# Two spreading transfers moved behind weight splits on ScalarE, and row products asked 0.9 sooner, in a hybrid decoder layer

## The chip, the cores and the metric

The kernel runs on 1 core of a Trainium2 chip. The metric is device time of one launch in microseconds (us); lower is better. The kernel before takes 1327.38 us, the median of 3 runs between 1325.91 and 1329.63.

The engines are named as the profile names them: PE is TensorE (matrix products), PEld its weight loads, DVE is VectorE, ACT is ScalarE, POOL is GpSimd, SP is SyncE. An engine name with a q (SPq, ACTq) is that engine's instruction queue where it issues a transfer (DMA). Each engine works through its own instructions in order, and engines wait for one another on semaphores.

## The reference

One decoder layer on 512 tokens of width 1024, in float32: a gated FFN, a mixer (a state-space scan with 16 heads in 4 groups beside differential attention with 8 heads), attention into a fixed memory of 256 rows, and a second gated FFN. Cut to the parts that the change touches:

```python
# differential attention: a learned bias per bucket of relative position, per head
bias = jnp.transpose(rel_bias[rel_bucket(rel)], (2, 0, 1))
logits = jnp.einsum('bqhcd,bkhcd->bhcqk', q_blk, k) * scale
logits = logits + bias[None, :, None]

# scan branch: a group norm over each of the 4 groups of channels
y = y.reshape(bsz, seqlen, SSD_WIDTH) * jax.nn.silu(z)
yg = y.reshape(bsz, seqlen, SSD_GROUPS, SSD_WIDTH // SSD_GROUPS)
yg = yg * lax.rsqrt(jnp.mean(yg * yg, axis=-1, keepdims=True) + EPS)

x = x + 0.5 * swiglu(rms_norm(x, norm_ffn1_w[l]), ffn1_w_in[l], ffn1_w_out[l])   # first FFN
```

## The kernel before

**Products in three passes.** Every large product takes both operands apart into a high and a low part and runs three passes on TensorE (high by high, low by high, high by low). A weight tile of 128x1024 (or 128x512) comes by a transfer from SyncE into one of six `wr` buffers; ScalarE writes the high part `wh` (L155), VectorE the low part `wl` (L156). This pair is called a weight split; three buffers each hold their results. TensorE can use a weight only when its split is done.

**The FFNs** use seven block products in place of eight. Some of them need sums of weight blocks. In the first FFN these sums are made on the way: GpSimd issues a second transfer that adds another block onto a `wr` buffer just loaded (L1290, "accumulating transfer"), or VectorE adds two loaded blocks (L1300, L1341). `out_blocks` (L1243) is the second half of a third of the FFN: seven products named here by their right operands, in the order "11" into `oa`, S1 into `oe`, S2 into `ob`, "12" into `oa`, S3 into `ob`, S4 into `oe`, "22" into `ob`. Each has, for the last third (3 tiles of the hidden width), a first part of 12 matmuls with a 128x1024 weight and a second part of 6 with a 128x512 weight; each part's split is asked for when the part begins. `recent` (L180, L1260) always holds the two instructions of the weight split asked for last.

**The order of the work.** A planner written by hand (`Order`, L57) emits the program. The dense products are one long generator; around them run chains (`spawn`), generators that yield how much later they want to go on. The planner's clock `od.t` advances with the matmuls emitted, by (columns + 8)/2400 us each for the three-pass kind and four times that for a plain float32 product. A chain resumes at the first step of the dense work at which its time has come. The numbers in `W` (L38 to L40) are such yields. SyncE's and GpSimd's instructions keep the order in which they are emitted (L104); the other engines' instructions are put in order by a scheduler that works from its own estimate of times and from data dependences. `tc.issue_after(i)` adds an order edge: what is traced inside it comes behind `i` on `i`'s engine; the kernel's helper `behind(ins)` (L184) does that for a list.

**The position table.** `prepare` (L604) is a chain spawned when the last third's `out_blocks` begins (`beside(2)`, L555). It loads the 32x8 table and a 32x512 one-hot matrix `hot`, and after 9.0 multiplies them on TensorE (`prel`, L614). After 1.5 ScalarE scales the result into `hot` (L619); after 2.0 ScalarE issues two small transfers to a table `rel_d` in device memory (L622, 8 KB each); after 6.0 it calls `expand_bias(S, hd)` for heads 0 and 1. `expand_bias` (L628) issues one transfer from the given queue that spreads a head's row of 640 values over 128 rows of `rel_z` (L629, 320 KB), from which `ask_bias` (L728) later reads a skewed 128x512 tile. The other six heads' spreads go out on SyncE in `queries_keys` (L738).

**The group norm.** `group` (L889) is a chain, one for each of the four groups of scan channels. At its end it sums squares with TensorE (`pn`), takes the root on GpSimd, waits `W["gn"]`, and calls `row_of(rh, 4, G, G, W["gr"])` (L992): VectorE splits the four columns, GpSimd makes two 128x512 diagonal tiles (`ndiag`, L368), the chain yields `W["gr"]`, and TensorE multiplies them by ones (`nrow`, L373, the "row products"). VectorE then scales `y` (L995), which is split for the output projection (`ysh`, `ysl`).

Of the kernel before, what the change touches and what calls it, by code (L numbers as in the profile page):

```python
# [35 lines left out]
LEAD = 4  # L36

W = {"h0": 3.4, "hs": 3.3, "hv": 2.08, "hp": 6.75}  # L38
W |= {"g0": 8.28, "gc": 0.75, "gx": 0.92, "gb": 2.59, "gs": 0.51, "gt": 2.0, "gd": 6.9, "gy": 0.38, "gq": 11.8, "gn": 1.5, "gr": 5.3}
W |= {"c0": 4.97, "cs": 3.0, "ct": 4.82}  # L40

SPLIT, AHEAD = 5, 2
# [58 lines left out]
def body(tc, a, dbg=None):  # L101
# [25 lines left out]
    def small(s, n, bufs=None):  # L127
        return tiny.tile([P, n], F32, tag=s, name=nm(s), bufs=bufs)
# [4 lines left out]
    def aux(s, shape=(P, T)):  # L133
        return aux_p.tile(list(shape), F32, tag="aux", name=nm(s))
# [5 lines left out]
    last, start, last_sum, recent, newest, newest_mm = [], [], [], [], [], []  # L140
    V, S, G = nc.vector, nc.scalar, nc.gpsimd
    od = Order()

    def mm(out, w, x, start, stop):
        od.t += (1 if w.dtype == R32 else 4) * (x.free_size() + 8) / 2400
        newest_mm[:] = [nc.tensor.matmul(out, w, x, start=start, stop=stop).ins]  # L146
# [36 lines left out]
    @contextmanager  # L183
    def behind(ins):  # L184
        with ExitStack() as after:
            for i in ins:
                after.enter_context(tc.issue_after(i))
            yield
# [361 lines left out]
    def beside(ti):  # L550
        if ti == 0:
            od.spawn(lambdas())
        elif ti == 1:
            od.spawn(early())
        elif ti == 2:  # L555
            od.spawn(prepare())
            od.spawn(memory_in(hm), 1.0)
# [46 lines left out]
    def prepare():  # L604
        rel_sb = small("rel_sb", 8, bufs=1)[:NUM_BUCKETS]
        nc.sync.dma_start(rel_sb, a["rel_bias"])
        for i in range(2):
            nc.sync.dma_start(hot[i], a["hot"][:, i * H : (i + 1) * H])
        rel_far = small("rel_far", 64, bufs=1)[:8]
        V.memset(rel_far, MASKED)  # L610
        yield 9.0
        prel = aux("prel", (8, T))
        for i in range(2):
            mm(prel[:, i * H : (i + 1) * H], rel_sb, hot[i], True, True)  # L614
        for c in range(T, RW, 64):
            S.dma_start(rel_d[:, c : c + 64], rel_far)
        yield 1.5
        for i in range(2):
            S.activation(hot[i][:8], prel[:, i * H : (i + 1) * H], AF.Copy, scale=-8.0)  # L619
        yield 2.0  # L620
        for i in range(2):
            S.dma_start(rel_d[:, i * H : (i + 1) * H], hot[i][:8])  # L622
        hot.clear()
        yield 6.0
        for hd in range(2):
            expand_bias(S, hd)

    def expand_bias(queue, hd):  # L628
        queue.dma_start(rel_z[hd, :, :RW], rel_d[hd : hd + 1].to_broadcast([P, RW]))  # L629
# [885 lines left out]
```

## Time and profile before

| | |
|---|---|
| median of 3 runs | 1327.38 us (1325.91 to 1329.63) |
| the profiled execution | 1329.7 us, of which the span of instructions is 1327.5 |
| mean granted TensorE clock | 0.991 |
| PE busy | 1298.4 us (98%) |
| DVE / ACT / POOL busy | 987.1 / 708.5 / 123.2 us |
| weight splits, ACT L155 | 329 of 1020 ns |
| weight splits, DVE L156 | 329 of 1174 ns |
| the two spreads from ScalarE, issue to landing | 5.4 us (median) |

In the profile, a row of the timeline or of the chain of waits has start, length, engine, line, operation, output<-inputs, count, and in brackets the idle time before it with what ended it. A row of the waits has the waiting engine, the line, what it waited for, then total, count and longest in us. A row of the stage table has the stretch, its length, then each engine's busy time (with its count), the granted TensorE clock as a share of full speed, the busy share of the 16 DMA engines and GB/s. Buffer numbers are left out of names.

### The profile page before, as it was taken

How to read it: one execution, taken by the hardware profiler on the slowest of the kernel's cores; microseconds unless marked ns; L12 is line 12 of the kernel's file. 1: busy time of each engine (PE TensorE's matmuls, PEld its weight loads, DVE VectorE, ACT ScalarE, POOL GpSimd, SP SyncE). 2: the span in 40 equal slices, each digit the busy share in tenths (PEclk: the TensorE clock that was granted, in tenths of full speed). 3: DMA queues.
4: the chain of work that ended last, by engine and by line, in shares of the span. 5: the costliest groups of instructions: out<-in, count | busy, mean ns of one | idle time of the engine just before them, and what ended most of it. 6: DMA issues, size and time to landing. Idle time of an engine off the chain costs nothing.

```text
span 1327.5 us, 20129 instructions
## 1 busy us (share of the span) xinstructions
PE 1298.4 (98%) x7724; PEld 1129.5 (85%) x7724; DVE 987.1 (74%) x1564; ACT 708.5 (53%) x1192; POOL 123.2 (9%) x143
## 2 busy tenths in 40 slices
PE   9999999998899999999999999999999999999996
PEld 7898998897787778777788877888889999989995
DVE  7988788787786586547867877645678878877886
ACT  6544555465654465336654556434465645555564
POOL 0001000010110011110111121120001000000001
PEclk9999999998899999999999999999999999999999
DMA  7567766885794533763465648775238876666752
GB/s 272 159 175 211 178 170 182 233 229 140 234 317 141 153 71 99 252 185 96 96 164 190 177 116 254 201 191 159 63 113 241 212 229 179 188 197 177 199 192 85
DMA packets 70127, 236.33 MB, mean 178 GB/s; under 512 B 8256, under 2 KB 9760, under 8 KB 69680
## 3 DMA queue, kind: packets, MB, share of 16 engines
q1 hardware_dynamic: 54352, 183.20, 40.8%
q0 software_dynamic: 12880, 44.62, 19.2%
q10 hardware_dynamic: 2800, 7.23, 1.7%
q8 instruction: 60, 0.98, 0.3%
q14 instruction: 35, 0.29, 0.1%
HBM read 232.87 MB, written 50.91 MB: 214 GB/s over the span
## 4 chain that ended last, share of the span: by engine, by line
PE 91%; DVE 3%; DMA 2%; ACT 1%; issue 1%; POOL 0%; ACTq 0%; POOLq 0%; DVEq 0%
PE qb L240 12%; PE pm L146 10%; PE qe L240 8%; PE qa L240 8%; PE pxbc L146 7%; PE ob L1270 6%; PE oe L1270 4%; PE oa L1270 4%; PE pq L146 4%; PE pk L146 3%; PE pcq L146 3%; PE pz L146 3%; PE pv L146 3%; PE pck L146 2%; PE pa L146 2%; DMA wr<-in_f1b 2%
## 5 line engine op out<-in xcount | busy, mean ns | idle before, releaser
L155 ACT ACTIVATE wh<-wr 128x1024 fp32r<-128x1024 f32 (+1 forms) x329 | 334.8, 1020 | 378.7 <-issue 66.5
L156 DVE TENSOR_TENSOR wl<-wr,wh 128x1024 fp32r<-128x1024 f32 (+1 forms) x329 | 385.3, 1174 | 151.9 <-ACT wh L155 149.7
L146 PE MATMUL pxbc<-hnh,wh 128*128 128x512 f32 x128 | 52.2, 408 | 0.0
L146 PE MATMUL pxbc<-hnh,wl 128*128 128x512 f32 x128 | 50.3, 393 | 0.0
L146 PE MATMUL pxbc<-hnl,wh 128*128 128x512 f32 x128 | 50.2, 392 | 0.0
L763 ACT ACTIVATE ec<-ec,mn 128x512 f32<-128x512 f32 (+3 forms) x64 | 35.4, 555 | 24.1 <-DVE mn L762 24.1
L240 PE MATMUL qe<-s31h,wl 128*128 128x256 f32 x152 | 43.1, 283 | 0.0
L240 PE MATMUL qa<-h11h,wh 128*128 128x256 f32 x152 | 43.1, 283 | 0.0
L240 PE MATMUL qb<-s24h,wh 128*128 128x256 f32 x152 | 43.0, 283 | 0.0
L240 PE MATMUL qb<-s24l,wh 128*128 128x256 f32 x152 | 43.0, 283 | 0.0
L240 PE MATMUL qb<-s24h,wl 128*128 128x256 f32 x152 | 43.0, 283 | 0.0
L240 PE MATMUL qa<-hmh,wh 128*128 128x256 f32 x152 | 43.0, 283 | 0.0
L240 PE MATMUL qa<-hml,wh 128*128 128x256 f32 x152 | 43.0, 283 | 0.0
L240 PE MATMUL qa<-hmh,wl 128*128 128x256 f32 x152 | 43.0, 283 | 0.0
L240 PE MATMUL qe<-s24h,wh 128*128 128x256 f32 x152 | 43.0, 283 | 0.0
L240 PE MATMUL qe<-s24l,wh 128*128 128x256 f32 x152 | 43.0, 283 | 0.0
L240 PE MATMUL qe<-s24h,wl 128*128 128x256 f32 x152 | 43.0, 283 | 0.0
L240 PE MATMUL qb<-hmh,wh 128*128 128x256 f32 x152 | 43.0, 283 | 0.0
L240 PE MATMUL qb<-hml,wh 128*128 128x256 f32 x152 | 43.0, 283 | 0.0
L240 PE MATMUL qb<-hmh,wl 128*128 128x256 f32 x152 | 43.0, 283 | 0.0
L240 PE MATMUL qa<-h11h,wl 128*128 128x256 f32 x152 | 43.0, 283 | 0.0
L240 PE MATMUL qa<-h11l,wh 128*128 128x256 f32 x152 | 43.0, 283 | 0.0
(448 smaller groups left out, 4184.3 us busy)
## 6 DMA issues: line engine op xcount, KB each, us to landing
wr<-in_f2q SPq DMA_DIRECT2D x44, 512.0 KB, 4.4
wr<-in_f1q SPq DMA_DIRECT2D x40, 512.0 KB, 4.5
wr<-in_f1b SPq DMA_DIRECT2D x30, 512.0 KB, 4.7
isum<-in_f2q SPq DMA_DIRECT2D x22, 512.0 KB, 5.9
wr<-isum SPq DMA_DIRECT2D x22, 512.0 KB, 4.7
wsum<-in_f2b SPq DMA_DIRECT2D x20, 512.0 KB, 6.1
wr<-wsum SPq DMA_DIRECT2D x20, 512.0 KB, 4.6
wr<-in_f1q POOLq DMA_DIRECT2D x16, 512.0 KB, 7.2
```

Source lines behind the costliest of these rows:

```text
L146: newest_mm[:] = [nc.tensor.matmul(out, w, x, start=start, stop=stop).ins]
L155: S.activation(hi, src, AF.Copy),
L156: V.tensor_tensor(lo, src, hi.bitcast(F32), ALU.subtract),
L240: newest_mm[:] = [nc.tensor.matmul(out, a_[:, wc], b_, start=first and f == 0 and kp == 0 and j == 0, stop=kp == n - 1 and j == 2, skip_gr ...
L763: S.activation(ec[:, :n], ec[:, :n], AF.Exp, bias=mn, scale=-1.0, accum_out=sm[c][:, i : i + 1])
L1270: newest_mm[:] = [nc.tensor.matmul(ps, a_[:, ts], b_[:, ws], start=first and k == 0 and j == 0, stop=k == n - 1 and j == 2, skip_group_che ...
```

## The change

`prepare`'s two calls of `expand_bias` now stand inside `behind(list(recent))`: each transfer is put behind the weight split asked for last at the time when it is emitted (its ScalarE half, since the transfer is issued by ScalarE). After each call the chain yields 4.0, so that the second is emitted at least 4.0 of the planner's time later. And `W["gr"]` falls from 5.3 to 4.4: the row products of the group norm are asked 0.9 of the planner's time sooner.

```diff
-W |= {"g0": 8.28, "gc": 0.75, "gx": 0.92, "gb": 2.59, "gs": 0.51, "gt": 2.0, "gd": 6.9, "gy": 0.38, "gq": 11.8, "gn": 1.5, "gr": 5.3}
+W |= {"g0": 8.28, "gc": 0.75, "gx": 0.92, "gb": 2.59, "gs": 0.51, "gt": 2.0, "gd": 6.9, "gy": 0.38, "gq": 11.8, "gn": 1.5, "gr": 4.4}
...
         hot.clear()
         yield 6.0
         for hd in range(2):
-            expand_bias(S, hd)
+            with behind(list(recent)):
+                expand_bias(S, hd)
+            yield 4.0
```

## Prediction

> **What bounds the kernel now.** I read the busy totals, then the chain that ended last as one line, to learn which engine to watch.
>
> ```profile
> PE 1298.4 (98%) x7724; PEld 1129.5 (85%) x7724; DVE 987.1 (74%) x1564; ACT 708.5 (53%) x1192; POOL 123.2 (9%) x143
> PE 91%; DVE 3%; DMA 2%; ACT 1%; issue 1%; POOL 0%; ACTq 0%; POOLq 0%; DVEq 0%
> ```
>
> TensorE is the bound nearly everywhere; ScalarE has 47% of the span to spare. The change adds and removes no instruction and no byte, so it can pay only where TensorE idles or runs at a lower clock. The waits of TensorE and of SyncE's queue say where (us in total, times, longest):
>
> ```profile
> PE oa L1270 <- ACT wh L155: 4.4, 2, 4.0
> PE pq L146 <- DVE vl L156: 3.1, 1, 3.1
> SPq L1251 <- DMA rel_d<-hot: 17.2, 1, 17.2
> ```
>
> The longest TensorE wait inside the kernel, 4.0 us, is for a weight split in the last output stage of the first FFN, where `prepare` works; the next, 3.1 us, comes right behind a group's row products. Both edits aim at a stall. The stage table shows the first (length, PE busy, PEld, DVE, ACT, POOL, granted clock, DMA share, GB/s):
>
> ```profile
> 320.00:324.19 4.19, 0.17 (x2) 0.01 (x1) 0.76 (x3) 1.27 (x3) 0.00 (x0) 0.68 0.26 46
> 324.19:328.40 4.21, 4.21 (x9) 2.94 (x10) 3.15 (x4) 2.37 (x4) 0.00 (x0) 0.51 0.96 286
> 328.40:338.60 10.20, 9.64 (x40) 6.98 (x38) 7.65 (x11) 3.39 (x6) 1.74 (x2) 1.00 0.75 188
> 338.60:343.30 4.70, 1.24 (x5) 0.61 (x5) 3.11 (x6) 4.38 (x8) 0.00 (x0) 0.86 0.49 165
> 343.30:348.50 5.20, 5.20 (x12) 4.16 (x13) 3.35 (x5) 1.63 (x6) 0.00 (x0) 0.50 0.59 197
> ```
>
> TensorE idles 4.02 + 0.56 + 3.46 = 8.0 us here, and two stretches at half clock lose 4.21 x 0.49 + 5.20 x 0.50 = 4.7 us. So 12.7 us is all that this stage can give. The chain of waits in time order, in this window, says what holds it (start, us, what):
>
> ```profile
> 320.20 0.65 ACT hot L619 x2
> ...
> 320.92 1.32 DMA rel_d<-hot
> ...
> 322.25 0.56 ACTq L629
> ...
> 322.85 0.61 ACTq L629
> ...
> 323.50 0.64 ACT wh L155
> ...
> 324.77 1.23 DVE wr L1300
> ...
> 326.02 5.74 DMA wr<-in_f1b
> ...
> 332.99 8.57 DMA wr<-in_f1b
> ...
> 341.65 0.16 ACT wh L155
> ...
> 342.19 1.05 ACT wh L155
> ...
> 343.28 2.08 PE oe L1270 x4
> ```
>
> The two spreading issues (L629) stand in ScalarE's queue ahead of a split. The first has to wait until the small table `rel_d` has landed, and the split stands behind both. The lateness then runs on: split, sum on VectorE (which frees a weight buffer), the fetch into that buffer, the accumulating transfer on top of it, and 18 us later the splits that TensorE waits for at 343.28.
>
> **Part 1: where the spreading transfers go.** `prepare` yields 9.0 + 1.5 + 2.0 + 6.0 = 18.5 of the planner's time after the last third's output products start. In that time the planner emits five products of 18 matmuls (520/2400 = 0.217 each, 3.9 a product) plus 0.88 for the table's own products; with rounding up to steps of 1.3 the first transfer is emitted at 20.4, just after the split of the second part of S3. The second, at least 4.0 later, follows the first split of the last product. So they go behind these two, in the ScalarE timeline:
>
> ```profile
> 341.65 1.58 ACT L155 ACTIVATE wh<-wr 128x512 fp32r<-128x512 f32 x2 [0.30 <-DMA wr<-in_f1b]
> 350.06 1.06 ACT L155 ACTIVATE wh<-wr 128x1024 fp32r<-128x1024 f32 x1 [0.99 <-PE ob L1270]
> ```
>
> Removed at 322: the wait and the two issues. The split at 323.50 can follow the small table's own issues directly; they start at 320.60 and end 0.62 later, at 321.22:
>
> ```profile
> 320.60 0.62 ACTq L622 DMA_DIRECT2D rel_d<-hot  x2
> 324.19 0.80 PE L1270 MATMUL oa<-wh,g11h 128*128 128x512 f32 x1 [4.02 <-ACT wh L155]
> 326.02 0.33 SPq L1251 DMA_DIRECT2D wr<-in_f1b  x1
> ```
>
> 323.50 - 321.25 = **2.25 us** sooner. TensorE starts at 321.9, so the first stall shrinks from 4.02 to 1.8. It does not vanish, for `rel_d` and its products stay put.
>
> What is late next: SyncE. Its fetches stood still for 17.2 us behind `rel_d` landing (row above), though they share no data with it; that transfer isn't moved, so fetching still resumes near 322. But the fetch at 326.02 follows the VectorE sum at 324.77, which follows the split: it moves 2.25 sooner too, to 323.8. It took 5.74 us while the 16 DMA engines were 0.96 busy, among others with the two spreads:
>
> ```profile
> wr<-in_f1b SPq DMA_DIRECT2D x30, 512.0 KB, 4.7
> rel_z<-rel_d ACTq DMA_DIRECT2D x2, 320.0 KB, 5.4
> ```
>
> Without 2 x 320 KB beside it I take the median of its kind, 4.7: 1.0 sooner. The ends are 0 (the other four fetches crowd as much) and 2.2 (640 KB at that stage's 286 GB/s). The accumulating transfer starts on its landing, so its end moves from 341.55 by 3.25.
>
> Added: the first issue now stands between the splits at 341.65 and 342.19. An issue is 0.56 to 0.61 long, and may begin while the activation before it still runs (320.60 above, while that of 320.20 ends at 320.85). The splits there stand 0.54 apart; 341.65 + 0.40 + 0.56 puts the next near 342.65, so TensorE's resumption at 343.28 gains 3.25 - 0.5 = **2.75 us**. The ends are 0, if another instruction takes that place, and 0.6, with nothing covering it. The second issue, after 350.06, lies beside ScalarE's squares, with TensorE busy throughout; without that cover it costs 0.6.
>
> Does the half clock of 343.30 to 348.50 go? Ends: 0, and 2.6 us back. The idles ahead of it:
>
> ```profile
> 339.72 0.50 PE L1270 MATMUL ob<-wh,s31h 128*128 128x512 f32 x1 [1.17 <-ACT wh L155]
> 343.28 0.80 PE L1270 MATMUL oe<-wh,s24h 128*128 128x512 f32 x1 [2.34 <-ACT wh L155]
> ```
>
> The first ends 3.25 sooner and the second 2.75, so the second stays about as long as it is. Half clock followed it; I take 0.
>
> Lateness of the spreads is harmless: the first reader of `rel_z` is issued at 382.1, and 350 + 0.6 + 5.4 is 356.
>
> ```profile
> L730 ACTq DMA_DIRECT2D bias<-rel_z x8: 326/326/612, 382.1 to 603.0; - x8
> 357.50:380.00 22.50, 22.48 (x189) 22.16 (x187) 20.25 (x36) 16.68 (x29) 7.86 (x7) 1.00 0.98 319
> ```
>
> Their 640 KB now lie just ahead of this DMA-full stretch: up to 640 KB / 319 GB/s = 2.0 us if the fetches had no lead. TensorE is never short there (22.48 of 22.50), so I take 0 and keep 2.0.
>
> **Part 2: row products 0.9 sooner.** The planner resumes a chain only between steps, and in the projections around it a step is three matmuls, 0.65: 5.3 is met at the ninth step (5.85), 4.4 at the seventh (4.55), so the products move 1.3, six matmuls. They read two products made on GpSimd; does TensorE then wait for these? First and last group:
>
> ```profile
> 566.09 1.04 POOL L368 TENSOR_TENSOR ndiag<-ident,cl 128x512 fp32r<-128x512 f32 x1
> 570.46 0.62 PE L146 MATMUL nrow<-ndiag,ones_r 128*128 128x512 f32 x2
> 830.17 1.04 POOL L368 TENSOR_TENSOR ndiag<-ident,cl 128x512 fp32r<-128x512 f32 x1
> 832.74 0.62 PE L146 MATMUL nrow<-ndiag,ones_r 128*128 128x512 f32 x2
> 576.22 0.50 PE L146 MATMUL pq<-hnh,wh 128*128 128x512 f32 x1 [3.06 <-DVE vl L156]
> 577.50:581.00 3.50, 3.50 (x10) 2.72 (x9) 0.45 (x1) 0.00 (x0) 0.00 (x0) 0.51 0.79 303
> ```
>
> Slack is 570.46 - 567.13 = 3.3 and 832.74 - 831.21 = 1.5: no wait, narrowly in the last. In the first group the row products feed `y` and its split, and these delay the value splits for which TensorE idles 3.06 us at 573 to 576. Six matmuls sooner gives **1.3 us**; ends 0 (the order on ScalarE or VectorE closes up differently) and 1.3. The half clock after it costs 3.50 x 0.49 = 1.7. An idle of 1.7 lies between 1.17 (before 339.72, no loss of clock) and 2.34: I take half, **0.85**. Other groups: 0, no stall follows them.
>
> [...]
>
> **Sum.** 2.75 + 1.3 + 0.85 = 4.9 us against the profiled execution's 1329.7 (span 1327.5 and 2.2 around it): 1324.8. That execution stands 2.3 above the median of the runs, 1327.38, so for a median I say **1322.5**.
>
> **Rivals.**
> (a) *The clock stays full.* The shorter gaps no longer trip it: 2.6 + 0.85 more come back, 1327.4 - 8.4 = 1319. For: 1.17 us did not trip it. Against: 2.34 did, and low activity began at 319, with the table's small products.
> (b) *The gain is swallowed.* SyncE stands behind `rel_d` until 322 as before, the fetches crowd, and the accumulating transfer lands when it did; TensorE waits at 339.72 instead of at 324.19. Only part 2's 1.3 stays: 1326. For: the 17.2 us row. Against: the chain puts the split, not SyncE, ahead of the fetch at 326.02.
> (c) *The edit moves nothing that counts*: other ScalarE work slides into the hole at 321 and the split stays near 323.5. 1326 to 1327.
> (d) *Slower.* SyncE's row shows that a DMA issue can wait for an unrelated earlier transfer. If the two moved issues do so inside the output stage, ScalarE stops for a fetch, 4.7 each, with two splits behind them: the one at 342.19, and this one, which is used 12 matmuls (2.7 us) after the last product's first:
>
> ```profile
> 353.05 0.62 ACT L155 ACTIVATE wh<-wr 128x512 fp32r<-128x512 f32 x1
> 353.27 0.39 PE L1270 MATMUL ob<-wh,gh 128*128 128x512 f32 x1
> ```
>
> The first costs TensorE 4.7; the second 4.7 less that split's lead, 353.27 + 2.7 - 353.67 = 2.3, so 2.4; a new half clock like the one at 324 costs 2.1. 9.2 - 2.25 - 1.0 - 1.3 = +4.6: 1332. It decides from about 4.4 us a wait. Against: fetches here come singly, so the transfer waited for would have to be a recent one.
>
> **How the numbers follow.** Chances: forecast 0.52, (a) 0.15, (b) 0.18, (c) 0.05, (d) 0.10. About 0.3%, 4 us, is what a measurement of this kernel tells from no change: faster means below 1323.4. Of the forecast's 0.52 I put 0.42 below that, as its own range 1320 to 1325 does; with (a), faster 0.57. Same: 0.10 + 0.18 + 0.05 = 0.33. Slower: 0.10. The range's low end is (a), with the fetch's full 2.2 (1.2 more), the issue for nothing (0.5) and the runs' scatter of 1.5 below their median: 1315.8. The high end is (b) and (c) with some 2 of scatter above: 1329. Outside lies (d), and little else.
>
> **What would show it.** Right: the split behind `rel_d`'s issues near 321.3; a first stall of about 1.8 us; the fetch of 326.02 near 323.8 and the accumulating transfer landing near 338; both L629 issues behind splits of this stage, without a wait; row products near 569 in a span shifted by 3, and an idle ahead of `pq` under 2 us. Wrong: a split still at 323.5; a ScalarE wait at either moved issue; a TensorE wait for GpSimd at row products; or TensorE short of weights from 357 to 380.

## The result and the profile after

| | before | after |
|---|---|---|
| median of the runs (lowest to highest), us | 1328.03 (1325.91 to 1329.63) | 1319.98 (1317.48 to 1320.33) |
| ratio, 95% interval | | 0.9936, 0.9917 to 0.9955 |
| profiled execution: time, span, granted clock | 1329.7, 1327.5, 0.991 | 1320.08, 1318.3, 0.994 |

The kernel became faster by 0.64%, 8 us of 1328. The forecast was 1322.5 in a range of 1315.8 to 1329.0, faster. A second comparison, against more runs of the kernel before, gave 0.9945 (0.9931 to 0.9959), that is 7.3 us (5.4 to 9.2), where the sum of the prediction says 4.9.

The lines of code behind the spreading transfers stand two lower after the change: L629 is L631, L1251 is L1253, L1270 is L1272. First the waits, of TensorE and of SyncE's queue (us in total, times, longest), in the changed kernel:

```profile
PE oa L1272 <- ACT wh L155: 1.8, 1, 1.8
PE oe L1272 <- ACT wh L155: 1.7, 2, 1.5
SPq L1253 <- DMA rel_d<-hot: 16.8, 1, 16.8
```

The 4.0 us stall of the output stage is 1.8 now. The row of `pq` waiting 3.1 us for `vl` is gone, and SyncE stands behind the small table as it did. The stage table of the changed kernel, cut at TensorE's two larger idles (length, PE busy, PEld, DVE, ACT, POOL, granted clock, DMA share, GB/s):

```profile
320.40:322.20 1.80, 0.01 (x2) 0.01 (x1) 0.60 (x2) 1.27 (x3) 0.00 (x0) 1.00 0.04 9
322.20:337.53 15.33, 14.37 (x52) 10.29 (x52) 11.98 (x17) 8.44 (x15) 1.73 (x2) 0.89 0.77 223
337.53:339.03 1.50, 0.00 (x2) 0.00 (x1) 1.50 (x3) 1.50 (x3) 0.00 (x0) 1.00 0.76 184
339.03:345.23 6.20, 6.08 (x19) 4.56 (x19) 4.82 (x8) 2.23 (x7) 0.00 (x0) 0.72 0.62 211
```

Idle is 1.79 + 0.96 + 1.50 + 0.12 = 4.4 us, where it was 8.0. At half clock 15.33 x 0.11 + 6.20 x 0.28 = 3.4 us are lost, where it was 4.7 in the two stretches of the prediction, and 6.8 with the part of the half clock that fell into the idles. The chain of waits of the changed kernel through the stage (start, us, what):

```profile
320.44 0.65 ACT hot L619 x2
...
321.51 0.64 ACT wh L155
...
322.20 1.24 PE oa L1272 x3
...
328.57 1.14 DVE wl L156
...
331.84 1.14 DVE wr L1343
332.98 0.60 DVE wl L156
...
334.79 1.05 ACT wh L155
```

The split follows the small table's issues directly, at 321.51, and neither the fetch nor the accumulating transfer stands on the chain any more, which runs over VectorE's work in their place. That holds for this execution: in e5, the same kernel once more, the chain runs over a fetch of 3.26 us and an accumulating transfer of 5.33 again. The second place, around the row products of the first group, in TensorE's and VectorE's timelines of the changed kernel:

```profile
564.46 0.62 PE L146 MATMUL nrow<-ndiag,ones_r 128*128 128x512 f32 x2
...
568.58 0.50 PE L146 MATMUL pq<-hnh,wh 128*128 128x512 f32 x1
```

```profile
567.84 1.28 DVE L156 TENSOR_TENSOR vl<-pv,vh 128x512 fp32r<-128x512 f32 x2
569.70 1.23 DVE L156 TENSOR_TENSOR wl<-wr,wh 128x1024 fp32r<-128x1024 f32 x1 [0.58 <-ACT wh L155]
```

`pq` follows the first value split without an idle. Two of the value splits `vl` now go ahead of the other weight split `wl`. Before, `wl` went first, in VectorE's timeline:

```profile
574.33 1.23 DVE L156 TENSOR_TENSOR wl<-wr,wh 128x1024 fp32r<-128x1024 f32 x1 [0.42 <-ACT wh L155]
575.48 2.48 DVE L156 TENSOR_TENSOR vl<-pv,vh 128x512 fp32r<-128x512 f32 x4
```

Cutting every profiled execution at the same four places shows where the time went. The first cut is the start of the table's products `prel`, the second that of `pxf`, which follows the output products, the third that of `pq`; half clock is the time spent in it within the first stretch. The experiments are described below.

| profile | `prel` to `pxf` | of it at half clock | `pxf` to `pq` | `pq` to the end |
|---|---|---|---|---|
| before | 38.22 | 13.7 | 218.86 | 751.28 |
| rows sooner alone (e2) | 36.30 | 10.2 | 215.77 | 749.86 |
| transfers moved alone (e1) | 33.76 | 6.8 | 219.05 | 751.51 |
| changed kernel | 33.11 | 6.8 | 216.09 | 749.72 |
| changed kernel again (e5) | 31.57 | 0 | 216.12 | 749.68 |

The first part of the change works in the first stretch alone. The second works in the other two: 2.7 to 3.1 us of idle ahead of `pq`, and 1.4 to 1.6 us of half clock behind it. What lies ahead of `prel` scatters by itself, between 319.1 and 320.5 in these five.

### The profile page after: what moved, and what is told of

Its sections match the earlier page's. It is cut to its first block, busy times and chain, and to the rows that moved or that the text cites. A ratio compares the mean times of both kernels' runs of the same rounds, so it can differ in the third digit from the quotient of the medians.

```text
span 1318.3 us, 20126 instructions
## 1 busy us (share of the span) xinstructions
PE 1294.9 (98%) x7724; PEld 1126.7 (85%) x7724; DVE 987.2 (75%) x1564; ACT 708.0 (54%) x1192; POOL 124.8 (9%) x143
## 4 chain that ended last, share of the span: by engine, by line
PE 91%; DVE 3%; ACT 2%; DMA 1%; issue 1%; POOL 0%; POOLq 0%; ACTq 0%; SPq 0%; DVEq 0%
PE qb L240 12%; PE pm L146 10%; PE qe L240 8%; PE qa L240 8%; PE pxbc L146 7%; PE ob L1272 6%; PE oe L1272 4%; PE oa L1272 4%; PE pk L146 3%; PE pq L146 3%; PE pcq L146 3%; PE pz L146 3%; PE pv L146 3%; PE pck L146 2%; PE pa L146 2%; PE pg L146 2%
```

## The experiments

**One part alone, e1 and e2.** The edit of e1 against the kernel before is the second hunk of the diff, that of e2 the first.

> The kernel before with the spreading transfers behind weight splits and the next step after each 4.0 later; row products stay at 5.3. Theory 1 (the two edits act at two separate places and add): the output stage gives back what it gave in the changed kernel, its end moving from 357.36 to about 352.5, and the first group's idle ahead of pq stays at 3.06 us; the time falls by 5.1 us of the span, a ratio of 0.9962 to 0.9966 against the kernel before (about 1323). Rival (the edits need each other: the earlier row products meet another order only because the stage ended sooner): the idle ahead of pq shrinks here too, and the time falls by 7 us or more, a ratio below 0.995.

> The kernel before with the row products asked at 4.4 in place of 5.3; the spreading transfers stay where they were. Theory 1 (the value splits now go ahead of the other weight split, so the whole idle ahead of pq and the half clock behind it go): the products nrow stand about 1.3 us sooner, vl goes ahead of wl, pq follows without an idle, and the time falls by 4.6 us, a ratio of about 0.9965 (about 1323.4). Rival (only the 1.3 us of the earlier products counts, as the prediction had it): the idle ahead of pq is 1.7 us, and the time falls by 1.3 to 2.2 us, a ratio of 0.998 to 0.999.

Measured: e1 0.9977 (0.9966 to 0.9989), 3.1 us (1.5 to 4.5) of 1327; e2 0.9968 (0.9956 to 0.9980), 4.2 us (2.7 to 5.8). Their product is 0.9945. In e1 the idle ahead of `pq` stays 3.06; in e2 it is gone and `wl` stands behind two of the value splits. TensorE's timeline of e1, then VectorE's of e2:

```profile
573.19 0.50 PE L146 MATMUL pq<-hnh,wh 128*128 128x512 f32 x1 [3.06 <-DVE vl L156]
```

```profile
570.50 1.28 DVE L156 TENSOR_TENSOR vl<-pv,vh 128x512 fp32r<-128x512 f32 x2
572.65 1.23 DVE L156 TENSOR_TENSOR wl<-wr,wh 128x1024 fp32r<-128x1024 f32 x1 [0.86 <-ACT wh L155]
```

Each part acts at its own place; e1 brought less than the 5.1 us that its theory expected. The 5.1 us that the stage lost from one profile to the other overstates the first part: e2 leaves the transfers where they were, and its stage is 1.9 us shorter than that of before all the same, with one piece of half clock fewer (10.2 us for 13.7). For the second part theory 1 holds, not the 1.3 us of the prediction.

**Is it the wait or the traffic? e3, e4 and e7.** Moving the transfers does two things: it frees ScalarE at 322, and it takes 640 KB out of the stretch in which fetches and accumulating transfers run. e3 issues the spreads from GpSimd's queue at the old time:

```diff
-        yield 6.0
         for hd in range(2):
-            expand_bias(S, hd)
+            expand_bias(G, hd)
```

> The kernel before with the two spreading transfers issued from GpSimd's queue at the old time, right behind the small table's writes; row products stay at 5.3. ScalarE is free of the issues, but the 640 KB still move during the output stage, and on GpSimd's queue they stand ahead of the accumulating transfers of the third part. Theory 1 (what counts is that the split no longer stands behind issues that wait for the small table): the split comes near 321.5, the first stall is 1.8 us in place of 4.0, and the stage ends 2 to 4 us sooner than before (ratio 0.997 to 0.9985), less than with the transfers moved away, since fetch and accumulating transfers stay near 5.7 and 8.6 us. Rival (what counts is that 640 KB leave this stretch): the first stall shrinks, yet the accumulating transfers land when they did before and the stage ends within 1 us of 357.4, a ratio of 0.999 to 1.001.

Measured: 1.0023 (1.0013 to 1.0033), 3.1 us slower. Waits of TensorE and the list of transfers of e3 in the stage (KB each, median us to landing):

```profile
PE ob L1269 <- ACT wh L155: 6.7, 1, 6.7
```

```profile
rel_z<-rel_d POOLq DMA_DIRECT2D x2, 320.0 KB, 8.2
wr<-in_f1b POOLq DMA_DIRECT2D x1, 512.0 KB, 7.9
...
wr<-in_f1b POOLq DMA_DIRECT2D x1, 256.0 KB, 8.5
```

The first stall is 1.80 us as in the changed kernel, and all of it is given back 20 us later, where TensorE waits 6.7 us for a split of weights that came late: the fetch ahead of it took 7.05 us and the accumulating transfer 7.90. Both theories of e3 missed the sign; the rival was nearer. e4 keeps the wait and moves the traffic:

```diff
         for hd in range(2):
-            expand_bias(S, hd)
+            S.dma_start(rel_s[hd, :, :64], rel_d[hd : hd + 1, :64])
+        for hd in range(2):
+            with behind(list(recent)):
+                expand_bias(S, hd)
+            yield 4.0
```

> The kernel before with the spreading transfers moved as in the change, and in their old place two transfers of 256 bytes each that read the small table as they do, so that ScalarE still stands behind the small table's landing; row products stay at 5.3. Two tiny transfers are added. Theory 1 (what counts is the wait ahead of the split): the split stays at 323.5, the first stall at 4.0 us, and the stage ends at most 2 us sooner than before, by the lighter traffic alone; ratio 0.9985 to 1.000. Rival (what counts is that 640 KB leave this stretch): the first stall stays at 4.0 us but fetch and accumulating transfer are as short as in the changed kernel, and the stage ends 3 us or more sooner; ratio 0.998 or below.

Measured: 1.0031 (1.0017 to 1.0045), slower, and neither theory had it. The two added transfers changed something else. Waits of SyncE's queue and of TensorE in e4, and its chain of waits:

```profile
SPq L1256 <- DMA rel_d<-hot: 21.0, 1, 21.0
PE oe L1275 <- ACT wh L155: 8.5, 2, 6.7
```

```profile
322.88 1.29 DMA rel_d<-hot
...
324.25 2.72 DMA wr<-in_f1b
...
327.53 7.47 DMA wr<-in_f1b
...
335.03 0.64 ACT wh L155
```

SyncE now stands 21.0 us behind the small table in place of 17.2, two fetches earlier in its list, and the first fetch held carries weights of the second product: TensorE waits 6.7 us for them. As a test of wait against traffic e4 tells nothing, but it shows that SyncE's wait can cost TensorE more than the stall that the change removed. e7 changes nothing but the transfers' place on ScalarE's own queue, so that they cross the accumulating transfers without holding a split:

```diff
-        yield 6.0
-        for hd in range(2):
-            expand_bias(S, hd)
+        with behind(list(recent)):
+            for hd in range(2):
+                expand_bias(S, hd)
```

> The kernel before with both spreading transfers issued on ScalarE behind the split at 327 in place of ahead of the one at 323.5; row products stay at 5.3. Nothing but their place on ScalarE's queue changes. Theory 2, formed on the run with GpSimd's queue (freeing ScalarE is worth nothing while the 640 KB cross the accumulating transfers): the first stall is 1.8 us, the accumulating transfers take 7 us or more, TensorE waits 3 us or more at the third part, and the stage from the table's products to the end of the output products is 36 to 39 us, as before; ratio 0.999 to 1.002. Rival (theory 1; the loss on GpSimd's queue was that queue's own, where a spread took 8.2 us): the stage is 34 to 35.5 us long; ratio 0.998 or below.

Measured: 0.9991 (0.9982 to 1.0001), 1.2 us. The stage is 35.93 us long, between the two expectations; ratio and accumulating transfers are those of theory 2. The list of transfers of e7:

```profile
rel_z<-rel_d ACTq DMA_DIRECT2D x2, 320.0 KB, 6.4
wr<-in_f1b POOLq DMA_DIRECT2D x1, 512.0 KB, 7.4
...
wr<-in_f1b POOLq DMA_DIRECT2D x1, 256.0 KB, 8.7
```

In the changed kernel the two accumulating transfers take 5.6 and 6.2 us, in e1 6.2 and 6.9. So freeing ScalarE is worth 1.2 us (-0.1 to 2.4) when the 640 KB cross these transfers, and 3.1 (1.5 to 4.5) in e1, where they move later; the two intervals overlap. This doesn't part wait from traffic in the kernel before. There the spreads, issued at 322.3 and 322.9 and landing at most 6.5 us later, are done before the accumulating transfers start at 332.4. These take 6.1 and 8.6 us before, but 5.4 and 6.5 in e2, where the spreads are at the same old place, and 5.3 and 7.5 in e5, where they are moved: one profile does not tell what the traffic does to them. The fetch ahead of them can be compared: on the chain of waits it takes 5.74 and 5.66 us with the spreads at the old place (before and e2), 4.53 and 4.60 with them later (e1 and e7). How much of e1's gain is wait and how much traffic stays open. With the traffic on GpSimd's queue the kernel is slower than before; the traffic also started 4 us earlier there than in e7, so that e3 and e7 do not separate the queue from the time.

**The order on VectorE, e5 and e6.** e5 is the changed kernel again; e6 asks for the row products at 5.0 in place of 4.4.

> The changed kernel once more, beside the next three. If the two edits only add, the ratio is the product of the two single ones, 0.9977 x 0.9968 = 0.9945, about 7 us of 1327; the stage from the table's products to the end of the output products is 32.5 to 34.5 us long. Rival (the edits help each other): a ratio of 0.993 or below.

> The changed kernel with the row products asked at 5.0 in place of 4.4: one step of three matmuls sooner than before, and the value splits stand behind the other weight split on VectorE, as before. Theory 1 (the order of the splits is what counts): the idle ahead of pq stays at 2.2 to 2.6 us and the half clock behind it too, so that this is 0.5 to 0.9 us better than moving the transfers alone and 3 us or more behind the changed kernel; ratio 0.997 to 0.998. Rival (only the earlier start of the products counts, and the clock stays full below some idle): the idle is 2.4 us with no half clock behind it, 2.3 us better than moving the transfers alone; ratio 0.996 or below.

Measured: e5 0.9945 (0.9931 to 0.9959), as the product, with a stage of 31.57 us, shorter than expected, as no half clock fell into it; e6 0.9949 (0.9933 to 0.9964), where the expectation of theory 1 was 0.997 or more. Its premise was wrong, not the mechanism: at 5.0 one value split had already got ahead. TensorE's and VectorE's timelines of e6:

```profile
562.33 0.62 PE L146 MATMUL nrow<-ndiag,ones_r 128*128 128x512 f32 x2
566.44 0.50 PE L146 MATMUL pq<-hnh,wh 128*128 128x512 f32 x1 [0.73 <-DVE vl L156]
```

```profile
565.70 0.68 DVE L156 TENSOR_TENSOR vl<-pv,vh 128x512 fp32r<-128x512 f32 x1
566.88 1.23 DVE L156 TENSOR_TENSOR wl<-wr,wh 128x1024 fp32r<-128x1024 f32 x1 [0.50 <-ACT wh L155]
```

From the start of `nrow` to that of `pq` it is 4.11 us in e6, 4.12 in the changed kernel (564.46 to 568.58), and 5.76 before (570.46 to 576.22). The order of the splits is therefore worth 1.64 us, alike in both. With the prediction's 0.65 for a step of three matmuls, one step and the order leave 3.06 - 0.65 - 1.64 = 0.77 of the idle, where 0.73 was measured; two steps and the order leave 0.1, and no idle of that size is left.

**SyncE's wait, e8 and e10, and what is left of the stall, e9 and e11.** e8 puts the small table's own two writes behind the split at 327 as well:

```diff
-        for i in range(2):
-            S.dma_start(rel_d[:, i * H : (i + 1) * H], hot[i][:8])
+        with behind(list(recent)):
+            for i in range(2):
+                S.dma_start(rel_d[:, i * H : (i + 1) * H], hot[i][:8])
```

> The changed kernel with the small table's own two writes put behind the split at 327 too, and the spreads 6.0 and 10.0 later as now. Theory (SyncE's fetch waits for the small table's landing though they share no data): the table lands near 329, the fetches that went out at 322.2 and 324 go out near 329, 5 us later, TensorE waits 4 us or more for the second or third part's weights, and the time is 4 us or more over the changed kernel's; ratio 0.998 or above. Rival (that wait is by chance and hides behind others): the first stall falls from 1.8 to 1.2 us and the time is the changed kernel's or 0.6 us less; ratio 0.9945 or below.

Measured: 0.9923 (0.9908 to 0.9937), 2.9 us below e5 (1316.94 against 1319.87): better than the changed kernel, where the theory said 4 us worse and the rival at most 0.6 us better. The later table did not hold SyncE longer; SyncE no longer waited for it at all. Its queue in e8 and then in the changed kernel (start, us, what):

```profile
306.22 0.33 SPq L1254 DMA_DIRECT2D wr<-in_f1b  x1
308.85 0.33 SPq L1254 DMA_DIRECT2D wr<-in_f1b  x1
```

```profile
304.97 0.33 SPq L1253 DMA_DIRECT2D wr<-in_f1b  x1
322.20 0.80 SPq L1253 DMA_DIRECT2D wr<-in_f1b  x2
```

Two fetches go out 13 to 16 us sooner. That the wait vanishes when the table's issue comes later on ScalarE fits a wait that follows from the order in which transfers are issued, not from data, but no view shown here names what they share, so this stays a reading. e10 makes the same edit to the kernel before; e9 adds to e8 the scalings of the table's products,

```diff
-        for i in range(2):
-            S.activation(hot[i][:8], prel[:, i * H : (i + 1) * H], AF.Copy, scale=-8.0)
+        with behind(list(recent)):
+            for i in range(2):
+                S.activation(hot[i][:8], prel[:, i * H : (i + 1) * H], AF.Copy, scale=-8.0)
```

and e11 asks in e8 for the table's products at 4.0 of the planner's time in place of 9.0.

> As the run in which the small table's writes stand behind the split at 327, and with ScalarE's two scalings of the table's products behind a later split as well, so that nothing of the table stands ahead of the first split. Theory (what is left of the first stall, 1.25 us, is the scalings and the wait for the products): the first stall falls below 0.3 us, the half clock behind it goes in most runs, 1.2 to 2.9 us less than that run; ratio 0.990 to 0.9915. Rival (TensorE then waits for the next split or for the fetch behind it): the stall moves to the second split; ratio 0.9915 to 0.993.

> The kernel before with the small table's two writes alone put behind the split at 327; the spreads, which have to follow them, come behind the next splits by themselves. Row products stay at 5.3. Theory (SyncE's fetches go out 16 us sooner, the first split is free, and the traffic is later): first stall 1.25 us, the stage from the table's products to the end of the output products 30 to 33 us, ratio 0.9945 to 0.9965, better than moving the spreads alone (0.9977). Rival (the release needs the spreads' own place too): SyncE waits for a spread in place of the small table, ratio 0.9977 or above.

> As the run in which the small table's writes stand behind a split, with the table's products asked at 4.0 in place of 9.0 of the planner's time, so that they stand among the output products and the writes and spreads come behind earlier splits. Theory (TensorE's small products no longer separate two output products, and the scalings wait for nothing): the first stall is 1.25 us less or gone from behind the products, but the spreads' 640 KB cross the accumulating transfers, which take 7 us or more; ratio 0.993 to 0.996, worse than that run's 0.9923. Rival (with fetches 16 us early the traffic no longer matters): ratio 0.9923 or below.

| | ratio, 95% interval | first stall, us | `prel` to `pxf`, us |
|---|---|---|---|
| e8 | 0.9923, 0.9908 to 0.9937 | 1.25 | 30.36 |
| e9 | 0.9909, 0.9894 to 0.9924 | 0.34 | 29.34 |
| e10 | 0.9960, 0.9947 to 0.9973 | 1.25 | 30.15 |
| e11 | 0.9924, 0.9908 to 0.9940 | 1.25 | 29.26 |

e10 is as its theory had it: the small table's writes alone bring 5.3 us (3.6 to 7.0). That includes what e1 does, since the first split is free and the spreads, which have to follow, go out at 333.7 and 339.2; over e1's 3.1 it is 2.2 us, beside e8's 2.9 over e5. e11 comes out as its rival said, level with e8: its products still stand behind the output products, and its accumulating transfers take 5.4 and 6.7 us. e9 is the fastest of all, 1315.15 us against 1327.01 of the kernel before in the same comparison, 12 us less; its first stall is nearly gone, its profile has no half clock in this stage, the ratio lies in the range of its theory (0.990 to 0.9915), and TensorE now waits longest in this stage for a split on VectorE. In TensorE's timeline of e9:

```profile
320.77 0.50 PE L1274 MATMUL oa<-wh,g11h 128*128 128x512 f32 x1 [0.34 <-ACT wh L155]
...
327.21 0.50 PE L1274 MATMUL oa<-wh,gh 128*128 128x512 f32 x1 [1.19 <-ACT wh L155]
...
337.03 0.50 PE L1274 MATMUL ob<-wl,s31h 128*128 128x512 f32 x1 [1.60 <-DVE wl L156]
```

The intervals of e8 and e9 overlap, and so do those of e8 and e5 and of e10 and e1, though all runs of e8 (1315.82 to 1318.88) lie below all of e5 (1319.24 to 1321.59); that of e9 (up to 0.9924) lies below that of e5 (from 0.9931), so that e9 beats both kernels.

## Why the prediction was right, step by step

- **Where the time is.** Right: both stalls named, and no other place changed. The other groups gained nothing: `pq` to the end fell by 1.6 us, which is the half clock behind the first group alone.
- **The split 2.25 us sooner.** Right: 321.51, first stall 1.79 for 1.8 forecast. The places of the two issues were right too, though the chain's steps in the output products are three matmuls, 0.65, and not 1.3: in e5 the first starts 0.08 us after the split it was to follow (338.73).
- **The fetch 1.0 us shorter.** Right in e1, where it takes 4.53 for 5.74. The accumulating transfer behind it was taken as fixed, and it is not: 6.22 in e1's chain of waits, 8.57 before, but 5.43 in e2 with the spreads unmoved, so its change can't be put down to the traffic. From the chain of e1:

```profile
325.03 4.53 DMA wr<-in_f1b
...
330.20 6.22 DMA wr<-in_f1b
```

- **The issue between the splits, -0.5.** Mixed: in the changed kernel's profile the issue started at 336.15, while activations ahead of the splits were still running, and cost nothing; in e5 it stands between the two splits as forecast and is on the chain, 0.56 us.
- **Half clock of the output stage, 0.** Wrong for the profile: 13.7 us at half clock became 6.8, and 0 in e5. The step took the half clock for a consequence of an idle's length; in e5 the clock stayed full after an idle of 2.35 us, as long as the 2.34 that half clock followed before.
- **First part, 2.75.** The sum is inside what e1 measured, 3.1 (1.5 to 4.5), though its terms are not all right.
- **Row products 1.3 us sooner.** Right in time, wrong in what it is worth. From `pxf` to `nrow` it is 213.3 us in e1 (354.14 to 567.44) and 212.0 in the changed kernel (352.49 to 564.46), 1.3 sooner. The step that failed is "ends 0 and 1.3 (the order on ScalarE or VectorE closes up differently)": the order was seen only as a way to lose. It was a way to win, 1.64 us, and the whole idle of 3.06 went.
- **Half of the half clock behind it, 0.85.** All of it went, 1.6.
- **Second part, 2.15.** Mis-sized: 4.2 (2.7 to 5.8) measured. This is the error of the forecast; 2.75 + 2.15 should have been near 2.75 + 3.0 + 1.6 = 7.4, and e5 measured 7.3.
- **Rivals.** (a) named 1319, near the 1319.98 measured, but the clock of the output stage did not stay full in that profile. (b) and (c) fell by the split at 321.51 and the shorter transfers. (d) did not come at either moved issue, yet what it describes, an issue that waits for an unrelated transfer, is what SyncE did all along (17.2 us before, 16.8 in the changed kernel), and moving the issues that it waited for was worth another 2 to 3 us by the medians (e10 over e1, e8 over e5). The 1319.98 lies nearer to (a) than to the forecast, but not for (a)'s reason: the difference is the second part.

## What to carry to other kernels

An instruction that comes a little sooner is worth the time by which it moves only if the queues behind it keep their order (here 1.3 us sooner, and 1.64 more from the order); look for the neighbour on each engine that it will now pass, and price that as a gain too. When a stall behind a DMA issue is removed, look where the moved traffic lands as well: here the freed split brought 1.2 us where the transfers crossed others and 3.1 where they went later, a difference that these runs do not yet make certain. And a queue's long wait for a transfer with which it shares no data (17.2 us here) deserves the first experiment, since moving two small issues brought some 2 to 3 us more here, by the medians.

## What the runs showed of the hardware

In these traces the half clock (a granted clock of 0.50) comes in pieces of 3.41 us on a fixed raster (a grid in time). In the changed kernel the two stretches of this stage run from 323.58 to 327.00 and from 340.65 to 344.06; their starts are 17.07 apart, five times 3.41. In the kernel before they start at 321.52 and 342.00, 20.48 or six times 3.413 apart, each two pieces long. The later stretches stand on the same raster: before at 577.52 and 1321.63, 69 and 218 pieces on, in the changed kernel at 1310.04, 284 pieces on. Counted from the start of the span it lies differently in the two executions: the first half clock begins 94 pieces and 0.67 us after it before, 94 pieces and 2.73 us in the changed kernel. Windows of the changed kernel on its own raster (the columns are those of the stage table):

```profile
320.17:323.58 3.41, 1.62 (x7) 0.87 (x6) 2.21 (x4) 1.39 (x5) 0.00 (x0) 1.00 0.09 23
323.58:326.99 3.41, 3.24 (x9) 2.04 (x8) 1.81 (x3) 3.41 (x7) 0.00 (x0) 0.50 1.00 350
337.24:340.65 3.41, 1.79 (x7) 0.97 (x6) 3.41 (x7) 3.36 (x8) 0.00 (x0) 1.00 0.43 104
340.65:344.06 3.41, 3.41 (x9) 2.65 (x8) 2.16 (x4) 0.53 (x1) 0.00 (x0) 0.50 0.72 255
```

The pieces with TensorE busy for 1.62 and 1.79 us were followed by half clock. The idles in them were 1.79 and 1.50 us long. An idle can also go free. Ahead of `pq`, in the kernel before and in e7, TensorE idles 3.06 us both times:

```profile
570.69:574.10 3.41, 2.47 (x11) 1.69 (x9) 2.75 (x4) 2.12 (x3) 0.81 (x1) 1.00 1.03 221
574.10:577.51 3.41, 1.29 (x6) 1.07 (x7) 3.18 (x5) 2.15 (x5) 0.00 (x0) 1.00 1.06 247
577.51:580.92 3.41, 3.41 (x10) 2.63 (x9) 0.44 (x1) 0.00 (x0) 0.00 (x0) 0.50 0.81 310
```

```profile
569.61:573.02 3.41, 2.05 (x9) 1.32 (x8) 2.94 (x5) 2.54 (x4) 0.81 (x1) 1.00 1.07 272
573.02:576.43 3.41, 1.71 (x7) 1.42 (x8) 3.41 (x5) 1.73 (x4) 0.00 (x0) 1.00 0.96 225
576.43:579.84 3.41, 3.41 (x16) 2.82 (x15) 0.03 (x1) 0.00 (x0) 0.00 (x0) 1.00 0.60 250
```

Before, one piece holds 2.12 us of the idle and half clock follows; in e7 it is split 1.36 and 1.70, and the clock stays full. e7's raster is not read off here but an estimate: it is carried on in steps of 3.413 us from e7's stretch at 323.87. Where a profile has no half clock in these stages (e5 and e9) it is carried back from the half clock at the end of that execution. At these two places, pieces at full clock with TensorE busy for 0.13 us (e10), 1.22 and 1.29 (before), and 1.62 and 1.79 (changed kernel) were followed by half clock; those busy for 1.71 (e7), 1.77 (e5), 1.81 (e9), 1.92 (e5 and e11), 2.05 us (e7) and longer were not. Left out here are the pieces that hold the table's small products (1.0 us or more of them): with TensorE busy for 2.05 (before), 2.16 (e10) and 2.17 us (e11) they were followed by half clock, and no view shown here says why. So a stall of 1.5 to 3 us cost nothing more in some of these profiles, and in others 1.7 us for each piece at half clock (3.41 x 0.50). This is a part of the scatter between executions: the changed kernel's stage had two pieces at half clock in one profile and none in the other, with idles as long (1.79 and 2.35 us in e5), and was 33.11 and 31.57 us long. A single profile's half clock should be priced as a chance, not as a term.
